# Row sums and scale spreading of the norms moved from VectorE to one-column and repeated-column products on TensorE

## The chip, the cores and the metric

The kernel runs on one core of a Trainium2 chip. The metric is the device time of one launch in microseconds (us). An engine is called by its short name in the profile: PE is TensorE's matmul (PEld its weight loads), DVE is VectorE, ACT is ScalarE, POOL is GpSimd, SP is SyncE, which here only issues DMAs.

## The reference

Two layers of a trunk on an activation `x` of 512 tokens by 1024 features, in float32. Per layer:

```python
x = x + 0.5 * swiglu(rms_norm(x, ffn1_norm), w_gate, w_up, w_down)     # D_FF 2816
h = rms_norm(x, mix_norm)
a, g, q, k, v = split(h @ w_in)
conv_out = silu(rms_norm(depthwise_conv31(a * sigmoid(g)) + conv_b, conv_norm))
diff_out = differential_attention(rms_norm(q), rms_norm(k), v, rel_bias, lam)   # 4 heads
x = x + concat(conv_out, diff_out) @ w_out
x = x + 0.5 * swiglu(rms_norm(x, ffn2_norm), w_gate, w_up, w_down)

def rms_norm(x, g):
    return x * rsqrt(mean(x * x, axis=-1) + 1e-6) * g
```

`lam` comes from four small vectors per layer: the exponentials of two dot products, and a constant.

## The kernel before

**Layout.** Features lie on the 128 partitions and tokens along the free axis: `x` is 8 tiles of 128 x 512. Most products are made three times (`mm3`, lines 160 to 167): weights and activations are split into a rounded high part (`whi`, `acth`, made by ACT or DVE) and the rest (`wlo`, `actl`), both in the format fp32r, and high x high, high x low and low x high are added up in PSUM. Weights come in through a ring of 5 raw buffers (`chunk`, `gather`, `sums`, lines 103 to 158). One product of 128 x 128 weights with 512 columns takes some 0.23 us of PE. Attention and its transposes use plain float32 products.

**The norms.** The gain of a norm goes into `acth` and `actl`; the scale of each token (one over the root of the mean square) is applied to the products afterwards. `Prep` (lines 252 to 275) squares each tile on ACT and adds the squares on POOL into `ssum` (128 x 512: one partial sum per partition and token). To get from there to a scale per token that every partition has, two helpers are used:

- `rows_rstd` (line 217) turns the 4 blocks of 128 tokens with 4 transposes on PE into PSUM, so that the tokens lie on partitions; DVE adds the 128 columns of each block (line 225), scales and adds epsilon (line 226); POOL raises to the power -0.5 (`rsqrt`, line 214). The result `rc` is 128 x 4: one number per token.
- `spread` (line 230) puts each column of `rc` on the diagonal of a 128 x 128 matrix (DVE, line 241) and multiplies a matrix of ones with it on PE (line 245), which leaves each token's scale in all partitions; ACT copies it to SBUF as `rb` (line 249). With `split=True` the number is first split into two fp32r parts (lines 234 and 236), two diagonals are made, and two fp32r products; else it is one product of 128 x 512 in float32.

Both are used eight times: for the four feed-forward blocks (split), for the input norm of the two mixers (not split), and for the norm over the channels of the convolution (`conv_finish`, line 690, not split), which sits in the last part of the mixer, where the last attention steps, the convolution's activation (tanh on ACT line 696, products on POOL line 694 and DVE lines 697 and 699) and the first output products meet.

**The order of the work.** Each engine works through its own queue in order. The order in each queue is not that of the Python text: a planner (`schedule_with_timeline_sim=True` in `kernel`) orders the instructions by its own estimate of when each can start, bound by data and by buffers: a tile with a `tag` and `bufs=n` has n buffers, and the next tile of the tag waits until an older one is done with. `keep_in_program_order` pins some instructions. In the very first feed-forward block the row sums are pinned before the fifth of eight accumulation steps of the third pair's first product group, and the spread before the fourth step of its second group (the call in `ffn`); in a mixer `first_products` pins both inside the second pair's products (`early`); in the three other feed-forward blocks and in `conv_finish` neither is pinned and the planner places them among the products.

**Buffers that the change touches.** The diagonals have the tag `diag` with one buffer (and a second one of the tag `sq`). The tile `lamv` of `make_scalars` (line 508 on) has the tag `diag` too. `make_scalars` is run once per layer's `lam`: a DMA from POOL's queue (line 513) spreads 4 x 64 numbers over all partitions, POOL multiplies (line 515, twice), DVE adds (line 517), ACT takes the exponential (line 519), DVE subtracts (line 521). `make_bias` (line 486 on) builds the table of the position bias with two small products (line 497), whose results DVE scales (line 498).

**The start.** Nine products of ones run while the first DMAs fly. Then `x` and the weights of the first two pairs arrive in three pieces (lines 189 to 198); ACT and DVE split them as they come, and PE follows.

Of the kernel before, what the change touches and what calls it, by code (L numbers as in the profile page):

```python
# [11 lines left out]
F32 = mybir.dt.float32  # L12
# [6 lines left out]
P = 128  # L19
# [48 lines left out]
def trunk(ctx: ExitStack, tc: tile.TileContext, xt, par, lamv, relb, onehot,  # L68
# [12 lines left out]
    def f32(ap):  # L81
        return ap.bitcast(F32)
# [3 lines left out]
    def bank(tag, name):  # L86
        return psum.tile([P, 512], F32, tag=tag, name=name, bufs=BANKS[tag])
# [124 lines left out]
    def rsqrt(v, n, use=""):  # L212
        y = small.tile([P, n], F32, tag=f"rs_y{n}{use}", name="rs_y")
        G.tensor_tensor(y, v, mhalf[:, :n], op=ALU.pow)
        return y

    def rows_rstd(s, dim, use="", pin=False):

        ps = bank("y", "ps_rows")
        for j in range(NT):  # L220
            mm = T.transpose(ps[:, j * P : (j + 1) * P], s[:, j * P : (j + 1) * P], ident)
            if pin:
                tc.keep_in_program_order(mm)
        v = small.tile([P, NT], F32, tag=f"rowv{use}", name="rowv")
        V.tensor_reduce(v, ps.rearrange("p (j c) -> p j c", j=NT), axis=AX.X, op=ALU.add)
        V.tensor_scalar(v, v, 1.0 / dim, EPS, op0=ALU.mult, op1=ALU.add)
        return rsqrt(v, NT, use), v

    def spread(rc, tag, pin=False, split=False):

        parts, dt, left = [rc], F32, ones
        if split:
            hi = small.tile([P, NT], F32R, tag="rc_hi", name="rc_hi")
            V.tensor_scalar(hi, rc, 1.0, None, op0=ALU.mult)
            lo = small.tile([P, NT], F32, tag="rc_lo", name="rc_lo")
            V.tensor_tensor(lo, rc, f32(hi), op=ALU.subtract)
            parts, dt, left = [f32(hi), lo], F32R, ones_r
        ps = bank("y", "ps_spread")
        for n, part in enumerate(parts):
            dg = tmp.tile([P, NT, P], dt, tag=("diag", "sq")[n], name="diag", bufs=1 + n)  # L240
            V.tensor_tensor(
                dg, ident.unsqueeze(1).broadcast_to([P, NT, P]),
                part.unsqueeze(2).broadcast_to([P, NT, P]), op=ALU.mult,
            )
            mm = T.matmul(ps, left, dg.rearrange("p j c -> p (j c)"), start=n == 0, stop=n == len(parts) - 1)
            if pin:
                tc.keep_in_program_order(mm)
        r = act.tile([P, SEQ], F32, tag=tag, name=tag)
        S.activation(r, ps, AF.Copy)
        return r  # L250

    class Prep:
# [30 lines left out]
    def products(pr, w, ps, i, at=None, amid=None):  # L283

        got = None
        for k in range(KT):
            if k == at:
                got = amid()
            mm3(ps, wpart(w[i], k), pr[k], k == 0, k == KT - 1, pin=at is not None and k in (0, at))
        return got  # L290
# [11 lines left out]
    def first_products(pr, w, ps, early=False):  # L302


        if not early:
            rc, v = rows_rstd(pr.s, DM)
            r = spread(rc, "rb", split=True)
        for k in range(KT):
            if early and k == STATS_AT:
                rc, v = rows_rstd(pr.s, DM, pin=True)  # L310
            for i in range(2):
                mm3(ps[0][i], wpart(w[0][i], k), pr[k], k == 0, k == KT - 1, pin=early and k in (0, STATS_AT))
        for i in range(2):
            for k in range(KT):
                if early and i == 0 and k == STATS_AT:
                    r = spread(rc, "rb", pin=True)
                mm3(ps[1][i], wpart(w[1][i], k), pr[k], k == 0, k == KT - 1, pin=early and k in (0, STATS_AT))
        return rc, v, r
# [95 lines left out]
    def ffn(pr, gu, dn, after, lead=None, aside=None):  # L414
        with tc.tile_pool(name="ffn", bufs=1) as fp:
            r = halves = None
            for m0, many in PARTS:
                hh, held, late = [], [], []

                def gated(n, us):  # L420
                    hi = fp.tile([P, SEQ], F32R, tag=f"hh{n}", name="hh")
                    lo = fp.tile([P, SEQ], F32R, tag=f"hl{n}", name="hl")
                    S.activation(hi, us, AF.Copy)
                    V.tensor_tensor(lo, us, f32(hi), op=ALU.subtract)
                    hh.append((hi, lo))

                def finish():
                    if late:
                        n, rest = late.pop()
                        gated(n, rest())  # L430

                for mm in range(many):
                    m = m0 + mm
                    if m == 4 and aside:
                        aside()
                    if m >= PLAIN:
                        w = sums(gu[m, 0], gu[m, 1])
                        late.append((mm, seven(halves, w, pair_banks(m), fp, finish, mm == many - 1)))
                        continue
                    w = lead[m] if lead and m < 2 else [chunk(gu[m, 0]), chunk(gu[m, 1])]  # L440
                    held.append((mm, w, pair_banks(m)))
                    if m == 0:
                        continue
                    if m == 1 and lead:
                        lead_products(pr, [h[1] for h in held], [h[2] for h in held])
                        continue
                    if m == 1:
                        _, _, r = first_products(pr, [h[1] for h in held], [h[2] for h in held])
                    elif r is None:
                        rc = products(pr, w, held[-1][2][0], 0, 4, lambda: rows_rstd(pr.s, DM, pin=True)[0])  # L450
                        r = products(pr, w, held[-1][2][1], 1, 3, lambda: spread(rc, "rb", pin=True, split=True))
                    else:
                        for i in range(2):
                            products(pr, w, held[-1][2][i], i)
                    for n, _, ps in held:
                        gs = fp.tile([P, 2, SEQ], F32, tag="gn", name="gs", bufs=2)
                        us = gs[:, 1]
                        V.tensor_tensor(gs[:, 0], ps[0], r, op=ALU.mult)
                        S.activation(gs[:, 0], gs[:, 0], AF.Silu)
                        V.tensor_tensor(us, ps[1], r, op=ALU.mult)  # L460
                        V.tensor_tensor(us, us, gs[:, 0], op=ALU.mult)
                        gated(n, us)
                    held = []
                    if not halves:
                        halves = Halves(fp, pr, r)
                finish()
                if m0 == 0:
                    halves.settle()
                blocks = [divmod(m0 + kk, HALF) for kk in range(many)]
                blocks = [(half, m * HALF + f) for m in range(KT) for half, f in blocks]  # L470
                w = None
                for m in range(KT):

                    ps = bank(turn_tag(m0 + many + m // 2), "ps_d")
                    for kk in range(many):
                        b = m * many + kk
                        if b % 8 == 0:
                            w = gather(dn, blocks[b : b + 8])
                        mm3(ps, wpart(w, b % 8), hh[kk], kk == 0, kk == many - 1)
                    V.scalar_tensor_tensor(x[:, m, :], ps, 0.5, x[:, m, :], op0=ALU.mult, op1=ALU.add)  # L480
                    if m0 + many == FT:
                        after(m)
# [58 lines left out]
    def mixer(l, pr, after):  # L541
        with tc.tile_pool(name="mix", bufs=1) as mp, tc.tile_pool(name="mt", bufs=2) as mt:
# [144 lines left out]
                conv_square(c, ys[c])  # L687

            def conv_finish():
                rcv = spread(rows_rstd(csum, CC, "c")[0], "rb")  # L690
                for c in range(CT):
                    z = ys[c]
                    hg = ghalf[l][:, c : c + 1]
                    G.tensor_tensor(z, z, rcv, op=ALU.mult)
                    th = mt.tile([P, SEQ], F32, tag="gl", name="th", bufs=1)
                    S.activation(th, z, AF.Tanh, scale=hg)
                    V.scalar_tensor_tensor(z, th, 1.0, z, op0=ALU.add, op1=ALU.mult)
                    S.activation(ch[:, c, :], z, AF.Copy, scale=hg)
                    V.scalar_tensor_tensor(cl[:, c, :], z, hg, f32(ch[:, c, :]), op0=ALU.mult, op1=ALU.subtract)
# [232 lines left out]
```

## Time and profile before

| | |
|---|---|
| median of 3 runs | 1796.49 us (1795.98 to 1796.54) |
| the profiled execution | 1796.31 us, its span 1794.5 us |
| PE busy | 1784.6 us, 99% of the span |
| DVE, ACT, POOL busy | 1211.1, 896.1 and 653.6 us |
| row sums' transposes (line 221) | 32 on PE |
| spread products (line 245) | 16 records on PE |
| sums on DVE (line 225) | 8 of 692 ns |
| diagonals on DVE (line 241) | 12 of 685 to 691 ns |
| ACT copy of the scale (line 249) | 8 of 598 ns |
| TensorE clock granted | full speed throughout |

A busy share is a share of the whole span. PE's ends are modelled and overlap, so PE's true pace is read from the distance between the starts of neighbouring products, not from the durations. A record in the tables is one instruction as the chip ran it; a float32 product appears as two of them.

### The profile page before, as it was taken

How to read it: one execution, taken by the hardware profiler on the slowest of the kernel's cores; microseconds unless marked ns; L12 is line 12 of the kernel's file. 1: busy time of each engine (PE TensorE's matmuls, PEld its weight loads, DVE VectorE, ACT ScalarE, POOL GpSimd, SP SyncE). 2: the span in 40 equal slices, each digit the busy share in tenths (PEclk: the TensorE clock that was granted, in tenths of full speed). 3: DMA queues.
4: the chain of work that ended last, by engine and by line, in shares of the span. 5: the costliest groups of instructions: out<-in, count | busy, mean ns of one | idle time of the engine just before them, and what ended most of it. 6: DMA issues, size and time to landing. Idle time of an engine off the chain costs nothing.

```text
span 1794.5 us, 28356 instructions
## 1 busy us (share of the span) xinstructions
PE 1784.6 (99%) x10845; PEld 1590.1 (89%) x10845; DVE 1211.1 (67%) x1863; ACT 896.1 (50%) x1482; POOL 653.6 (36%) x460
## 2 busy tenths in 40 slices
PE   9999999999999999999999999999999999999999
PEld 7899899888788899899888998998887888998997
DVE  6976477568867867477576765765788587673762
ACT  6555265445744456256433643654558354552651
POOL 4242232269843132133102312412797331322420
PEclk9999999999999999999999999999999999999999
DMA  7466476323212366466333654663231133664651
GB/s 243 107 179 183 108 181 176 118 94 94 71 48 83 94 165 188 106 171 189 105 94 98 171 167 120 177 179 118 71 114 51 48 106 91 166 178 112 180 150 59
DMA packets 111721, 231.24 MB, mean 129 GB/s; under 512 B 12151, under 2 KB 33414, under 8 KB 111584
## 3 DMA queue, kind: packets, MB, share of 16 engines
q1 hardware_dynamic: 91488, 191.93, 33.4%
q0 software_dynamic: 19808, 37.33, 12.5%
q8 instruction: 85, 1.39, 0.3%
q14 instruction: 52, 0.43, 0.1%
q10 hardware_dynamic: 288, 0.16, 0.0%
HBM read 227.26 MB, written 3.42 MB: 129 GB/s over the span
## 4 chain that ended last, share of the span: by engine, by line
PE 96%; DVE 2%; issue 1%; ACT 1%; DMA 0%; SPq 0%; ACTq 0%; DVEq 0%
PE ps_pair L384 38%; PE ps_d L166 9%; PE ps_d L163 9%; PE ps_d L167 9%; PE ps_pair L167 5%; PE ps_pair L166 5%; PE ps_pair L163 5%; PE ps_pair L596 2%; PE ps_pair L597 2%; PE ps_pair L598 2%; PE ps_out L163 1%; PE ps_out L166 1%; PE ps_sc L714 1%; PE ps_out L167 1%; DVE actl L263 1%; PE ps_v L628 1%
## 5 line engine op out<-in xcount | busy, mean ns | idle before, releaser
L100 ACT ACTIVATE whi<-wraw 128x1024 fp32r<-128x1024 f32 (+2 forms) x599 | 465.9, 802 | 609.5 <-PE ps_pair L384 225.7
L101 DVE TENSOR_TENSOR wlo<-wraw,whi 128x512 fp32r<-128x512 f32 (+2 forms) x556 | 526.0, 968 | 212.6 <-ACT whi L100 208.4
L384 PE MATMUL ps_pair<-acth,wlo 128*128 128x256 f32 x1088 | 308.5, 284 | 0.0
L384 PE MATMUL ps_pair<-actl,whi 128*128 128x256 f32 x1088 | 308.5, 284 | 0.0
L384 PE MATMUL ps_pair<-acth,whi 128*128 128x256 f32 x1088 | 308.4, 283 | 0.0
L166 PE MATMUL ps_d<-hl,whi 128*128 128x512 f32 x704 | 274.2, 390 | 0.0
L167 PE MATMUL ps_d<-hh,wlo 128*128 128x512 f32 x704 | 273.4, 390 | 0.0
L163 PE MATMUL ps_d<-hh,whi 128*128 128x512 f32 x704 | 268.7, 390 | 0.0
L384 PE MATMUL ps_pair<-th,wlo 128*128 128x256 f32 x816 | 231.3, 283 | 0.0
L384 PE MATMUL ps_pair<-tl,whi 128*128 128x256 f32 x816 | 231.2, 283 | 0.0
L384 PE MATMUL ps_pair<-th,whi 128*128 128x256 f32 x816 | 231.2, 283 | 0.0
L146 POOL TENSOR_TENSOR wraw<-wraw 128x512 f32<-128x512 f32 x68 | 101.8, 1497 | 339.5 <-DMA wraw<-in_gu 272.2
L141 POOL DMA_DIRECT2D wraw<-in_gu x68 | 82.0, 1207 | 392.4 <-DMA wraw<-in_gu 228.6
L384 PEld LDWEIGHTS ps_pair<-acth,whi 128*128 128x128 f32 x1088 | 209.1, 192 | 0.3
L384 PEld LDWEIGHTS ps_pair<-actl,whi 128*128 128x128 f32 x1088 | 209.0, 192 | 0.3
L384 PEld LDWEIGHTS ps_pair<-acth,wlo 128*128 128x128 f32 x1088 | 209.1, 192 | 0.0
L480 DVE SCALAR_TENSOR_TENSOR x<-ps_d,x 128x512 f32<-128x512 f32 x96 | 64.7, 689 | 179.6 <-PE ps_d L167 179.3
L166 PE MATMUL ps_pair<-actl,whi 128*128 128x512 f32 x448 | 175.0, 391 | 0.3
L163 PE MATMUL ps_pair<-acth,whi 128*128 128x512 f32 x448 | 174.4, 394 | 0.5 <-ACT whi L100 0.3
L167 PE MATMUL ps_pair<-acth,wlo 128*128 128x512 f32 x448 | 174.5, 391 | 0.0
L384 PEld LDWEIGHTS ps_pair<-tl,whi 128*128 128x128 f32 x816 | 156.7, 192 | 0.7
L384 PEld LDWEIGHTS ps_pair<-th,whi 128*128 128x128 f32 x816 | 156.7, 192 | 0.6
(176 smaller groups left out, 3268.9 us busy)
## 6 DMA issues: line engine op xcount, KB each, us to landing
wraw<-in_gu SPq DMA_DIRECT2D x208, 256.0 KB, 4.0
wraw<-in_gu SPq DMA_DIRECT2D x104, 512.0 KB, 3.7
wraw<-in_gu POOLq DMA_DIRECT2D x68, 512.0 KB, 5.7
wraw<-in_wqkv SPq DMA_DIRECT2D x24, 512.0 KB, 3.7
wraw<-in_dn SPq DMA_DIRECT2D x84, 128.0 KB, 3.1
wraw<-in_dn SPq DMA_DIRECT2D x32, 256.0 KB, 3.1
wraw<-in_wag SPq DMA_DIRECT2D x16, 512.0 KB, 3.6
wraw<-in_wout SPq DMA_DIRECT2D x16, 512.0 KB, 3.6
```

The lines of the kernel that those rows point to most:

```text
L100: S.activation(hi, raw, AF.Copy)
L101: (eng or V).tensor_tensor(out=lo, in0=raw, in1=f32(hi), op=ALU.subtract)
L141: nc.gpsimd.dma_start(two.rearrange("p (b c) -> p b c", b=2), u[:, h[0]].unsqueeze(1).broadcast_to([P, 2, 512]), accum_op=ALU.add)
L146: G.tensor_tensor(more[:, h[0]], two[:, h[1]], whole[:, h[0]], op=ALU.add)
L163: first = T.matmul(ps, wh, xh, start=start, stop=False)
L166: T.matmul(ps, wh, xl, start=False, stop=False)
L167: T.matmul(ps, wl, xh, start=False, stop=stop)
L384: mm = T.matmul(ps, l, r, start=first and i == j == 0, stop=False, skip_group_check=True)
L480: V.scalar_tensor_tensor(x[:, m, :], ps, 0.5, x[:, m, :], op0=ALU.mult, op1=ALU.add)
L596: T.matmul(ps[n], xh[:, t], wh, start=k == 0, stop=False)
L597: T.matmul(ps[n], xh[:, t], wl, start=False, stop=False)
L598: T.matmul(ps[n], xl[:, t], wh, start=False, stop=k == KT - 1)
```

## The change

`rows_rstd` no longer transposes: for each block of 128 tokens the block of `ssum` is the stationary operand and a single column of ones is streamed through, which sums over the partitions and leaves 128 x 1 in PSUM. DVE then reads 128 x 4 instead of 128 x 512, and the sum on DVE (line 225) falls away. `spread` makes no diagonals and no split: for each block the column of `rc`, repeated 128 times by its access pattern, is the stationary operand and the identity matrix (128 x 128) is streamed through; four float32 products of 128 columns take the place of one or two of 512. The scale, epsilon, power and the ACT copy stay. The tag `diag` is then used by `lamv` alone.

```diff
-    def rows_rstd(s, dim, use="", pin=False):
-        ps = bank("y", "ps_rows")
+    def rows_rstd(sums, dim, use="", pin=False):
+        ps = bank("y", "ps_rows")[:, :NT]
         for j in range(NT):
-            mm = T.transpose(ps[:, j * P : (j + 1) * P], s[:, j * P : (j + 1) * P], ident)
+            for n, s in enumerate(sums):
+                mm = T.matmul(ps[:, j : j + 1], s[:, j * P : (j + 1) * P], ones[:, :1],
+                              start=n == 0, stop=n == len(sums) - 1)
+                if pin:
+                    tc.keep_in_program_order(mm)
+        v = small.tile([P, NT], F32, tag=f"rowv{use}", name="rowv")
+        V.tensor_scalar(v, ps, 1.0 / dim, EPS, op0=ALU.mult, op1=ALU.add)
+        return rsqrt(v, NT, use), v
+    def spread_bank(rc, pin=False):
+        ps = bank("y", "ps_spread")
+        for j in range(NT):
+            mm = T.matmul(ps[:, j * P : (j + 1) * P], rc[:, j : j + 1].broadcast_to([P, P]), ident, start=True, stop=True)
             if pin:
                 tc.keep_in_program_order(mm)
-        v = small.tile([P, NT], F32, tag=f"rowv{use}", name="rowv")
-        V.tensor_reduce(v, ps.rearrange("p (j c) -> p j c", j=NT), axis=AX.X, op=ALU.add)
-        V.tensor_scalar(v, v, 1.0 / dim, EPS, op0=ALU.mult, op1=ALU.add)
-        return rsqrt(v, NT, use), v
-    def spread(rc, tag, pin=False, split=False):
-        parts, dt, left = [rc], F32, ones
-        if split:
...
-            parts, dt, left = [f32(hi), lo], F32R, ones_r
-        ps = bank("y", "ps_spread")
-        for n, part in enumerate(parts):
-            dg = tmp.tile([P, NT, P], dt, tag=("diag", "sq")[n], name="diag", bufs=1 + n)
-            V.tensor_tensor(
-                dg, ident.unsqueeze(1).broadcast_to([P, NT, P]),
-                part.unsqueeze(2).broadcast_to([P, NT, P]), op=ALU.mult,
-            )
-            mm = T.matmul(ps, left, dg.rearrange("p j c -> p (j c)"), start=n == 0, stop=n == len(parts) - 1)
-            if pin:
-                tc.keep_in_program_order(mm)
+        return ps
+    def spread(rc, tag, pin=False):
         r = act.tile([P, SEQ], F32, tag=tag, name=tag)
-        S.activation(r, ps, AF.Copy)
+        S.activation(r, spread_bank(rc, pin), AF.Copy)
         return r
...
-            r = spread(rc, "rb", split=True)
+            r = spread(rc, "rb")
...
-                        r = products(pr, w, held[-1][2][1], 1, 3, lambda: spread(rc, "rb", pin=True, split=True))
+                        r = products(pr, w, held[-1][2][1], 1, 3, lambda: spread(rc, "rb", pin=True))
...
-                rcv = spread(rows_rstd(csum, CC, "c")[0], "rb")
+                rcv = spread(rows_rstd([csum], CC, "c")[0], "rb")
```

More of the change, by code (lines that the diff above doesn't have):

```diff
@@ L227, in rows_rstd @@
-        return rsqrt(v, NT, use), v
-    def spread(rc, tag, pin=False, split=False):
-        parts, dt, left = [rc], F32, ones
-        if split:
[L233 to L236, printed above, removed]
-            parts, dt, left = [f32(hi), lo], F32R, ones_r
-        ps = bank("y", "ps_spread")
-        for n, part in enumerate(parts):
-            dg = tmp.tile([P, NT, P], dt, tag=("diag", "sq")[n], name="diag", bufs=1 + n)
-            V.tensor_tensor(
-                dg, ident.unsqueeze(1).broadcast_to([P, NT, P]),
-                part.unsqueeze(2).broadcast_to([P, NT, P]), op=ALU.mult,
-            )
-            mm = T.matmul(ps, left, dg.rearrange("p j c -> p (j c)"), start=n == 0, stop=n == len(parts) - 1)
-            if pin:
-                tc.keep_in_program_order(mm)
+        return ps
@@ L305, in first_products @@
         if not early:
-            rc, v = rows_rstd(pr.s, DM)
-            r = spread(rc, "rb", split=True)
+            rc, v = rows_rstd([pr.s], DM)
+            r = spread(rc, "rb")
         for k in range(KT):
             if early and k == STATS_AT:
-                rc, v = rows_rstd(pr.s, DM, pin=True)
+                rc, v = rows_rstd([pr.s], DM, pin=True)
             for i in range(2):
@@ L449, in ffn @@
                     elif r is None:
-                        rc = products(pr, w, held[-1][2][0], 0, 4, lambda: rows_rstd(pr.s, DM, pin=True)[0])
-                        r = products(pr, w, held[-1][2][1], 1, 3, lambda: spread(rc, "rb", pin=True, split=True))
+                        rc = products(pr, w, held[-1][2][0], 0, 4, lambda: rows_rstd([pr.s], DM, pin=True)[0])
+                        r = products(pr, w, held[-1][2][1], 1, 3, lambda: spread(rc, "rb", pin=True))
                     else:
```

## The prediction

> **What bounds the kernel now.** I read the busy shares first, then the chain of work that ended last, then the rows of the two helpers, and last the few stretches where PE isn't gapless. The shares and the chain, from the page:
>
> ```profile
> span 1794.5 us, 28356 instructions
> ...
> PE 1784.6 (99%) x10845; PEld 1590.1 (89%) x10845; DVE 1211.1 (67%) x1863; ACT 896.1 (50%) x1482; POOL 653.6 (36%) x460
> ...
> PE 96%; DVE 2%; issue 1%; ACT 1%; DMA 0%; SPq 0%; ACTq 0%; DVEq 0%
> ```
>
> PE carries 96% of the chain, so a PE instruction put among the products costs its full spacing, and DVE work taken away is worth nothing except where DVE holds PE up. What the helpers cost PE is read from distances between starts. The first row sums (timeline, PE):
>
> ```profile
> 31.27 0.39 PE L167 MATMUL ps_pair<-acth,wlo 128*128 128x512 f32 x1
> 31.50 0.60 PE L221 MATMUL ps_rows<-ident,ssum 128*128 128x128 f32 x4
> 31.86 0.48 PE L163 MATMUL ps_pair<-acth,whi 128*128 128x512 f32 x1
> 32.17 0.39 PE L166 MATMUL ps_pair<-actl,whi 128*128 128x512 f32 x1
> ```
>
> From 31.27 to 32.17 are 0.90 us; two regular products at 0.23 leave 0.44 for four transposes, 0.11 each. Pieces of the chain give the other spacings:
>
> ```profile
> 36.90 0.73 PE ps_spread L245 x2
> 91.72 76.31 PE ps_pair L384 x636
> 370.40 0.86 PE ps_spread L245 x2
> 477.82 0.89 PE ps_o L744 x8
> ```
>
> The split spread took 0.73 at its first place (two products of 0.23 and a wait for a diagonal; at the other three feed-forward blocks they sit 0.23 apart from their neighbours, 0.46 in all); the float32 spread 0.86; eight records of a float32 product of 128 columns (four products) 0.89, 0.111 a record; a product of 256 columns 0.120.
>
> Not gapless are the start and the last part of each mixer. At the start (timelines of ACT, POOL and PEld, and the row of the `lamv` DMA):
>
> ```profile
> 13.22 2.67 ACT L100 ACTIVATE whi<-wraw 128x512 fp32r<-128x512 f32 x4
> 15.93 2.08 ACT L262 ACTIVATE acth<-x,par 128x512 fp32r<-128x512 f32 x3
> ```
> ```profile
> 26.37 1.06 ACT L100 ACTIVATE whi<-wraw 128x1024 fp32r<-128x1024 f32 x1 [0.51 <-PE ps_pair L166]
> ```
> ```profile
> 29.08 0.19 PEld L167 LDWEIGHTS ps_pair<-acth,wlo 128*128 128x128 f32 x1 [0.45 <-DVE wlo L101]
> ```
> ```profile
> DMA to landing us min/median/max: 3.5/3.5/3.6
> ```
>
> ACT works without a gap from 13.22 to 20.5, then squares at POOL's pace, and the split at 26.37 feeds the weights for which PE stands at 29.08: ACT is only 0.51 us ahead there. The mixer's end (busy time by stretch: stretch, length, PE, PEld, DVE, ACT, POOL, clock, DMA share, GB/s):
>
> ```profile
> 490.00:500.00 10.00, 9.71 (x67) 8.00 (x66) 9.79 (x37) 7.94 (x27) 4.59 (x5) 1.00 0.00 0
> 500.00:512.00 12.00, 10.49 (x58) 7.96 (x58) 12.00 (x39) 9.85 (x28) 4.63 (x6) 1.00 0.01 1
> ```
>
> DVE is full. At the spacings above, PE's instructions from 489.85 to 512.2 (22.35 us) come to 18.8 us, so PE loses some 3.5 us there, mostly to the convolution's steps (the longest, 1.26 us, at 501.73 for `acth`, line 698). The second mixer has the same figures at 1381 to 1403.
>
> **The change part by part.** The sum is made against the profiled execution, 1796.31 us (span 1794.5 and 1.8 around it; 0.18 under the median).
>
> *Row sums on PE.* Four transposes (0.44) become four float32 products, each with two weight loads of 128 columns and one column streamed: eight records. No row shows one column. Low end: from 256 to 512 columns a record grows by 0.108 (0.120 to 0.228), so it would shrink to 0.012 at one column, 0.1 in all: -0.34 a place. High end: loads don't overlap and each takes the 0.19 us of its own record: 1.52, +1.08 a place. I take 0.111, the spacing of transposes and of 128-column records alike: the nearest rows, equal though the work streamed differs, which points to the load as the floor. 0.89, +0.45 a place. Six places lie in gapless PE: +2.7 (-2.0 to +6.5). The two in `conv_finish` are counted below.
>
> The Trainium skill's page "TensorE: Matmul & The Clock Gate", section "Back-to-back issue gap", gives about 60 cycles, or 25 ns, for 1 to 64 columns in an isolated stream. By it, as an estimate, a place would cost 0.2 instead of 0.89, the six 1.4 less than before, and the total +0.3 instead of +4.4. No record here has fewer than 128 columns on full weights.
>
> *Spread on PE.* Four float32 products of 128 columns: 8 x 0.111 = 0.89. First block 0.73 to 0.89, +0.16; three feed-forward blocks 0.46 to 0.89, +1.29; two mixers 0.86 to 0.89, +0.06. Sum +1.5 (a repeated column as weights isn't in the trace; I take it for a load like any other. Low end 0.86 a place, which the same columns took as one float32 product: +1.3; high end 0.19 a record: +5.3).
>
> *DVE.* Gone are 8 sums of 0.69, 12 diagonals of 0.69 and 8 small splits of 0.17: 15 us. Outside `conv_finish` PE's products cover them, and the scale just comes 1.4 to 2.2 us earlier to a spread that is pinned or waits its turn: nothing. The cover isn't lost.
>
> *`conv_finish`.* Here DVE and the latency count: sum and diagonal were 1.38 us, the timeline's rows at 490.54 and 493.29. In the compiled order the spread also stands three value products and a group of transposes earlier, and ACT's copy two instructions earlier. I work the scale's copy out at 494.9 instead of 496.34: rows end 0.45 later, DVE's small step waits behind `ov` to 491.7, power to 492.8, spread behind one score product to 494.7. All four channels follow it one by one some 2.5 us apart, so the gain of 1.4 arrives, less 0.2 for products pushed back: -1.2 a mixer, -2.4. Ends: all 1.7 us of latency (-3.4) or the rows' extra 0.45 uncovered and no gain (+0.9).
>
> *The start: `lamv` moves.* With the diagonals gone nothing holds its buffer, and the planner moves both layers' chains from 37 to 58 us to the very start. On POOL two DMA issues (0.58 each), four products (0.65 each) before the squares' sums; on DVE two sums (0.28) and two differences (0.14); on ACT two exponentials (0.20), behind the first three and the eighth of the weight splits. SP's queue is unchanged; ACT loses two table loads of 1.28 at 49 to 54, which covers nothing PE waits for; the bias product (0.95) moves ahead of the spread, its input issued one POOL instruction earlier: nothing.
> First chain: POOL is free at 6.1, products to 7.45, DVE's sum to 7.8, exponential to 8.05 instead of ACT going on at 6.37. ACT catches up by 10.8, since the next tile lands at 11.2 whatever it does. Nothing, but 128 KB ahead of that tile at some 300 GB/s: +0.3.
> Second chain: POOL reaches the DMA issue at 10.3. It lands in 3.5 us by the row above; the engines were then 60% busy, here 100% (1.04 of share, 400 GB/s from 12 to 20), where `x` took 5.4: I take 4.4. Then 1.3 for products, 0.3 sum, 0.4 for exponential and signals: 16.7. ACT stands before it from 13.9, 2.8 us late; less the 0.51 ahead, PE's wait at 29.08 grows by 2.3. Queued behind DVE's sum are four `wlo` and three `actl`, behind ACT's exponential three `whi` and three `acth`, then all squares; PE reaches them just late enough (17.5 on). With the 0.3, +2.6. Ends: landing in 1.9 (the fastest on POOL's queue, `oneh`) 0.3; in 5.7 (the median of POOL's large ones) 3.9.
>
> Sum: +2.7 +1.5 -2.4 +2.6 = +4.4; 1796.31 + 4.4 = 1800.7 us.
>
> **The rivals.**
> A. *A one-column product is cheap* (the low end). For it: the slope with columns. Against: the equal 0.111 of transposes and 128-column records. -2.0 in place of +2.7: 1796.0, no slower. It decides once a record costs under 0.02 us; below 0.094 the loss is under 0.2%. The page's rule above, 25 ns, would be this rival.
> B. *DVE's relief empties the mixers' ends.* DVE is full in just the 22 us where PE loses 3.5. If all of it comes back, -7.1 in place of -2.4: 1796.0, no slower. Against: the four channels run one after another on one `th` buffer, so only the start moves. It decides where a mixer gains over 3.4.
> C. *Loads don't overlap* when nothing streams between them: 0.19 a record, 6.5 in place of 2.7: 1804.5. Against: every row's spacing is under its load's 0.19.
> D. *The start doesn't stall*, the second `lamv` lands within 2 us: 1798.4. For it: `oneh` did. Against: both `lamv` rows, on a less busy DMA.
>
> **How the numbers follow.** Forecast 56%, its own range 1797.5 to 1804; A 14%, B 12%, C 10%, D 8%. A difference under 0.2% (3.6 us) is about what a measurement tells from none. Slower than 1800.1: 0.7 of the forecast and all of C, 0.49. Faster than 1792.9: a third of A and a fifth of B, 0.07. Same: the rest, 0.44. The range leaves out C's upper half and the faster thirds of A and B: 1795 to 1804.5.
>
> **What would show it.** Starts in the changed trace: eight one-column records taking about 0.9 us out of the stream (A 0.1, C 1.5); spread 0.89 everywhere; ACT idle before the second exponential until 16 to 17 us and PE's wait near 29 grown to about 3; `rb` in the mixer's end 1.4 us nearer to its row sums. Wrong would make me most of all a one-column record far from 0.11, or the planner's new order in the mixers' ends, where attention and convolution interleave differently, costing or saving more than the 1.2 worked out.

## The result and the profile after

The changed kernel takes 1802.57 us (median of 6 runs, 1802.33 to 1804.19), the kernel before 1796.45 beside it: ratio 1.0038, 95% interval 1.0028 to 1.0048, so 6.1 us slower. The forecast was 1800.7 with a range of 1795.0 to 1804.5. The profiled execution of the changed kernel is the slowest of the six, 1804.19 with a span of 1802.4, and has a stretch of half clock at the start, told below; its granted clock is 0.999, that of the other five, which lie between 1802.33 and 1803.08, is 1.000.

Page of the changed kernel, span, busy shares and chain by engine:

```profile
span 1802.4 us, 28487 instructions
...
PE 1790.9 (99%) x10925; PEld 1600.3 (89%) x10925; DVE 1201.6 (67%) x1835; ACT 894.3 (50%) x1480; POOL 646.3 (36%) x460
...
PE 94%; DVE 3%; ACT 1%; issue 1%; POOL 1%; DMA 1%; ACTq 0%; DVEq 0%; POOLq 0%
```

PE has 80 records more and is busy 6.3 us longer; DVE's busy time fell by 9.5 us (the forecast had 15) without making the kernel shorter. The chain of work that ended last, first of the changed kernel, then of before, each cut to pieces that have a counterpart in the other:

```profile
96.18 76.31 PE ps_pair L378 x636
...
...
482.80 0.89 PE ps_o L738 x8
551.01 1.22 DVE wlo L101
641.80 76.31 PE ps_pair L378 x636
989.18 76.31 PE ps_pair L378 x636
```
```profile
546.23 1.22 DVE wlo L101
636.14 76.31 PE ps_pair L384 x636
982.62 76.31 PE ps_pair L384 x636
```

The first two pieces start at 91.72 and 477.82 in the chain of before. The differences are where the time came from:

| stretch | distance to before at its end | grew by | forecast |
|---|---|---|---|
| start, with the first block's row sums and spread | +4.46 | 4.46 | 3.2 |
| first mixer's row sums and spread | +4.98 | 0.52 | 0.48 |
| first mixer's end (`conv_finish`) | +4.78 | -0.20 | -1.2 |
| second feed-forward block | +5.66 | 0.88 | 0.88 |
| next layer's first feed-forward block | +6.56 | 0.90 | 0.88 |

The second layer repeats it: +0.55 in the mixer's front, -0.10 in its end, +0.87 in the last block. The mixers' fronts and the feed-forward blocks are as forecast. The mixers' ends are not, and the start has 1.3 more than forecast in this one execution.

**Row sums and spread in gapless PE** (timeline of the changed kernel, PE, start and duration):

```profile
366.49 0.39 PE L167 MATMUL ps_pair<-acth,wlo 128*128 128x512 f32 x1
366.72 0.95 PE L223 MATMUL ps_rows<-ones,ssum 128*128 128x1 f32 x8
367.53 0.49 PE L163 MATMUL ps_pair<-acth,whi 128*128 128x512 f32 x1
367.85 0.40 PE L166 MATMUL ps_pair<-actl,whi 128*128 128x512 f32 x1
```

From 366.49 to 367.85 are 1.36 us; less two regular products of 0.23 the eight one-column records took 0.90, 0.11 each. The forecast had 0.89, from records of 128 columns.

**The start** (changed kernel: row of the `lamv` DMA, ACT and PE from the timelines):

```profile
DMA to landing us min/median/max: 4.1/5.1/6.1
```
```profile
16.73 0.20 ACT L513 ACTIVATE lame<-lamd 128x2 f32<-128x2 f32 x1 [3.31 <-DVE lamd L511]
```
```profile
27.80 0.39 PE L167 MATMUL ps_pair<-acth,wlo 128*128 128x512 f32 x1
29.18 0.51 PE L163 MATMUL ps_pair<-acth,whi 128*128 128x512 f32 x1 [0.99 <-ACT whi L100]
29.52 0.39 PE L166 MATMUL ps_pair<-actl,whi 128*128 128x512 f32 x1
31.36 0.50 PE L167 MATMUL ps_pair<-acth,wlo 128*128 128x512 f32 x1 [1.45 <-DVE wlo L101]
31.70 0.50 PE L163 MATMUL ps_pair<-acth,whi 128*128 128x512 f32 x1
32.00 0.63 PE L166 MATMUL ps_pair<-actl,whi 128*128 128x512 f32 x1
32.43 0.63 PE L167 MATMUL ps_pair<-acth,wlo 128*128 128x512 f32 x1
```

ACT stands 3.31 us before the second exponential and PE waits 0.99 and 1.45 us for the weight splits that come behind it, 2.4 in all (before: 0.45 at 29.08). The last two lines stand 0.43 apart where regular products stand 0.23 apart, and so it goes on to 34.99: PE at about half its pace for 3 us. The granted clock from 32 to 35 is 0.50. The ten products from 31.36 to the row sums at 35.35 took 3.99 us, where the run with the move alone, below, needed 2.39 for ten: 1.6 us lost, which more than covers the 1.3.

### The profile page after: what moved, and what is told of

The parts are those of the page before. It is cut to its first block, busy times and chain, and to the rows that moved or that the text cites. A ratio compares the mean times of both kernels' runs of the same rounds, so it can differ in the third digit from the quotient of the medians.

```text
span 1802.4 us, 28487 instructions
## 1 busy us (share of the span) xinstructions
PE 1790.9 (99%) x10925; PEld 1600.3 (89%) x10925; DVE 1201.6 (67%) x1835; ACT 894.3 (50%) x1480; POOL 646.3 (36%) x460
## 4 chain that ended last, share of the span: by engine, by line
PE 94%; DVE 3%; ACT 1%; issue 1%; POOL 1%; DMA 1%; ACTq 0%; DVEq 0%; POOLq 0%
PE ps_pair L378 38%; PE ps_d L166 9%; PE ps_d L163 9%; PE ps_d L167 9%; PE ps_pair L167 5%; PE ps_pair L166 5%; PE ps_pair L163 5%; PE ps_pair L591 2%; PE ps_pair L592 2%; PE ps_pair L590 2%; PE ps_sc L708 1%; PE ps_out L163 1%; PE ps_out L167 1%; PE ps_out L166 1%; DVE actl L257 1%; PE ps_v L622 1%
```

## The experiments

All medians are against the kernel before on the same chip: 1796.09 for the first four runs, 1796.05 for the next seven, 1796.20 for the last.

**The parts apart.** First the move of the scalars' chains alone, on the kernel before:

```diff
-SPACE = 392
+SPACE = 376
...
-            t = tmp.tile([P, SEQ], F32, tag="diag", name="lamv", bufs=1)
+            t = tmp.tile([P, 6 * HD], F32, tag="lamv", name="lamv", bufs=1)
```

> The kernel before with one edit: lamv gets a buffer of its own (SBUF was 64 bytes too full for it, so the bias table's spare columns shrink from 392 to 376), so that the chains of both layers' scalars start at the very beginning as in the changed kernel; row sums and spread stay as they were. Forecast's step: the second lamv transfer holds up ACT's weight splits and PE's wait near 29 us grows by some 2.3, in all +2.6 over the kernel before. From the changed kernel's trace: its first long group starts 4.46 later, of which 0.6 are the first block's row sums and spread and some 1.6 a stretch of half clock in that execution, so +2.3, and about +3.9 in an execution with the slow stretch. Rival (the move is free, the time at the start comes from something else, such as the helpers' new order): +0.3 or less.

Measured: 1798.83, +2.7 (ratio 1.0016, 1.0007 to 1.0025). Its chain passes the first long group at 93.79 and keeps that distance of 2.0 to 2.1 to before to the end, and it contains the transfer and the splits behind it:

```profile
9.35 6.03 DMA lamv<-in_lamv
16.67 1.57 ACT whi L100 x3
```

The profiled execution took 1798.33. Three of the eleven show a granted clock of 0.999 and took 1799.59 to 1800.43, which points to the half clock in some executions here too. The move costs 2.0 to 2.7 without any of the new products; the rival that it is free falls.

Next, the changed kernel with the chains held back by another buffer:

```diff
-            t = tmp.tile([P, SEQ], F32, tag="diag", name="lamv", bufs=1)
+            t = tmp.tile([P, SEQ], F32, tag="sq", name="lamv")
```

> The changed kernel with one edit: lamv takes a buffer of the squares' rotation instead of the diagonals' unused one, which holds the scalars' chains back until squares are done; everything else is as in the change. If the move costs 2.3 to 2.6 by itself, this is the changed kernel less that: +3.6 to +3.9 over the kernel before, and no half clock at the start, since PE never stands still long enough. By the forecast's sum, whose conv_finish term was -2.4, it would be +1.8. Rival (the move is free): as the changed kernel, +6.1.

Measured: 1799.99, +3.9 (1.0022, 1.0014 to 1.0031): 2.2 less than the whole change, and not the +1.8 of the forecast's sum. The first mixer's end got 0.17 shorter by its chain (478.86 and 547.10 stand at +1.04 and +0.87).

The new row sums alone, with the scalars' chains where the diagonals hold them before, and the new spread alone, with the chains behind the squares. One of the eight places in each run; the comments say which functions stand there:

```python
rcv = spread(rows_rstd([csum], CC, "c")[0], "rb")   # row sums alone: new rows_rstd, old spread
...
rcv = spread(rows_rstd(csum, CC, "c")[0], "rb")     # spread alone: old rows_rstd, new spread
```

> The kernel before with the new row sums alone (one-column products with ones in all eight places); the spread by diagonals stays and with it the place of the scalars' chains. Forecast: six gapless places at +0.45 are +2.7; in conv_finish DVE's sum of 0.69 goes and PE pays 0.45, so 0 to -0.5 for both mixers, together +2.2 to +2.7. From the changed kernel's trace (0.90 us a place out of the stream where transposes took 0.44; mixers' ends hardly gaining): +2.7 to +3.0. Rival A (one column is cheap): -2. Rival (the two parts hinder each other and neither costs this alone): under +2.

> The kernel before with the new spread alone (repeated columns of weights times the identity in all places), the old row sums by transposes and DVE, and the scalars' chains held back as in the run with them held. Forecast: +1.5 in gapless places (0.16 at the first block, 0.43 at three feed-forward blocks, 0.03 at two mixers), and in conv_finish the diagonal's 0.69 off the latency, -0.7 a mixer, together about +0.1. From the changed kernel's trace, whose mixers' ends got only 0.1 to 0.2 shorter with both parts, of which the row sums' extra 0.45 is in the way: +0.3 to +1.3. The sum of this run and of the one with row sums alone should be that of the run with the chains held, if the parts add.

Measured: row sums 1797.91, +1.8 (1.0010, 1.0002 to 1.0019); spread 1797.25, +1.2 (1.0006, 0.9997 to 1.0015). The sum, 3.0, is 0.9 under the run with both; the intervals reach 1.6 us to either side, so the times alone don't show that the parts fail to add. By the chains the places agree with their price of 0.45 and 0.43 in the feed-forward blocks (636.54 and 983.49 in the chain of the row sums stand at +0.40 and +0.87, 636.10 and 983.02 in that of the spread at -0.04 and +0.40), and the first mixer's end gained 0.27 with the row sums, 0.22 with the spread, and 0.17 with both (the second 0.20, 0.13 and 0.07): the two gains don't add. That is 0.3 a mixer of the 0.9. The rest lies at the start, and single profiles don't settle it: the first group of 636 starts at 91.72 in the profile of before, and at 91.75, 91.36 and 91.31 in three runs below that differ from it only in the mixers.

**What prices a record.** One column against 128 columns, on the run with the chains held:

```diff
-        ps = bank("y", "ps_rows")[:, :NT]
+        ps = bank("y", "ps_rows")
...
-                mm = T.matmul(ps[:, j : j + 1], s[:, j * P : (j + 1) * P], ones[:, :1],
+                mm = T.matmul(ps[:, j * P : (j + 1) * P], s[:, j * P : (j + 1) * P], ones,
...
-        V.tensor_scalar(v, ps, 1.0 / dim, EPS, op0=ALU.mult, op1=ALU.add)
+        V.tensor_scalar(v, ps[:, ::P], 1.0 / dim, EPS, op0=ALU.mult, op1=ALU.add)
```

> As the run with the scalars' chains held, with one edit: the row sums' products stream all 128 columns of ones instead of one, and VectorE reads every 128th column of the result; still eight records a place. If the loads of the 128-column weights set a record's price, the eight cost 8 x 0.111 (the spread's records) instead of 8 x 0.099, +0.1 a place, +0.6 to +0.8 over the run with the chains held. Rival A's slope (a record shrinks with its columns, from 0.108 less per 256 columns) would make a one-column record 0.054 shorter than a 128-column one: 0.43 a place, +2.6 in six places.

Measured: 1799.91 against 1799.99 (+3.86 and +3.90, each over the kernel before beside it). Its PE timeline:

```profile
362.40 0.39 PE L167 MATMUL ps_pair<-acth,wlo 128*128 128x512 f32 x1
362.63 1.05 PE L223 MATMUL ps_rows<-ones,ssum 128*128 128x128 f32 x8
363.44 0.48 PE L163 MATMUL ps_pair<-acth,whi 128*128 128x512 f32 x1
363.75 0.40 PE L166 MATMUL ps_pair<-actl,whi 128*128 128x512 f32 x1
```

1.35 us from 362.40 to 363.75, as with one column (1.36). From 1 to 128 columns the streamed columns cost nothing; rival A's slope falls. Each record has its own load of 128 columns of weights in both variants, and that is what they have in common; a run with narrower weights was not made. The only narrower loads in the trace of before, four columns for the bias, take 0.08 us against 0.19, but the two records of 128 columns that go with two of them took 0.31 us together (53.26 to 53.57), not less than 0.11 each. So that the load sets the price is argued, not shown.

**Why the start pays.** The changed kernel with a second buffer for the second layer's `lamv`:

```diff
-SPACE = 392
+SPACE = 376
...
-            t = tmp.tile([P, SEQ], F32, tag="diag", name="lamv", bufs=1)
+            t = tmp.tile([P, SEQ if l == 0 else 6 * HD], F32, tag="diag" if l == 0 else "lamv", name="lamv", bufs=1)
```

> The changed kernel with one edit: the second layer's lamv has a buffer of its own, so that its transfer is issued right behind the first instead of after the first chain's sums (the bias table's spare columns shrink from 392 to 376 for the space). The chains stay at the very start. Forecast's mechanism (ACT stands before the second exponential because that transfer is issued at 9.5 to 10.3 and lands at 15.6): it lands by about 12, ACT hardly waits, and 1.8 to 2.5 of the 2.6 at the start go; total +3.6 to +4.3 over the kernel before, and no half clock. Rival (the start pays for the extra instructions and the 128 KB each ahead of the weights): as the changed kernel, +6.1.

Measured: 1800.08, +4.0 (1.0021, 1.0011 to 1.0031), where the whole change was +6.1. ACT's exponentials (timeline):

```profile
9.28 0.19 ACT L513 ACTIVATE lame<-lamd 128x2 f32<-128x2 f32 x1
11.57 0.19 ACT L513 ACTIVATE lame<-lamd 128x2 f32<-128x2 f32 x1
```

No idle time stands before either, PE is gapless from 24 to 32 us, and the first long group starts at 92.26, 0.54 behind before, which is the first block's row sums and spread (0.61 by the forecast). The chains are still at the very start and work as much; the second transfer left POOL at 2.5 instead of 9.5 (the planner also put PE's first products in a slightly different order). So it was the late transfer that made the move dear, not its instructions.

**The mixers' ends.** The disputed term by itself: the new row sums and spread (`rows_new`, `spread_new`) in `conv_finish` alone, on the kernel before:

```diff
-                rcv = spread(rows_rstd(csum, CC, "c")[0], "rb")
+                rcv = spread_new(rows_new([csum], CC, "c")[0], "rb")
```

> The kernel before with the change made in conv_finish alone: one-column row sums and the new spread there, everything else as before. This is the term that the forecast put at -1.2 a mixer, -2.4 in all: 1793.7. From the chains of the runs with everything changed and the scalars' chains held, whose mixers' ends got 0.17 and 0.12 shorter: -0.3, 1795.8.

Measured: 1795.96, -0.1 (1.0001, 0.9992 to 1.0010); by its chain the two ends are 0.17 and 0.06 shorter. The -2.4 falls: the interval's low end is -1.4. But the scale did come earlier. ACT's timeline in this run, the scale's copy, the first channel's tanh and the last channel's `acth`:

```profile
495.30 0.61 ACT L278 ACTIVATE rb<-ps_spread 128x512 f32<-128x512 f32 x1
...
497.68 0.72 ACT L725 ACTIVATE th<-yp,ghalf 128x512 f32<-128x512 f32 x1
...
508.75 0.72 ACT L727 ACTIVATE acth<-u,ghalf 128x512 fp32r<-128x512 f32 x1
```

The same three in the timeline of before:

```profile
496.34 0.58 ACT L249 ACTIVATE rb<-ps_spread 128x512 f32<-128x512 f32 x1
...
498.80 0.73 ACT L696 ACTIVATE th<-yp,ghalf 128x512 f32<-128x512 f32 x1
...
509.36 0.72 ACT L698 ACTIVATE acth<-u,ghalf 128x512 fp32r<-128x512 f32 x1 [0.90 <-DVE u L697]
```

The surroundings stand at the same place within 0.04 (the value products of 477.82 at 477.86). So the scale is 1.04 earlier, the first channel 1.12, the last only 0.61. And PE's waits from 489 to 513 (the view of waits; engine, line, what it waited for, total, times, longest), of before and of this run:

```profile
PE ps_out L163 <- ACT acth L698: 1.3, 1, 1.3
PE ps_o L744 <- ACT at L737: 0.2, 1, 0.2
```
```profile
PE ps_out L163 <- DVE mn L747: 0.6, 1, 0.6
PE ps_at L764 <- ACT at L766: 0.2, 1, 0.2
```

The wait of the first output product for the convolution's `acth` is gone; in its place that product waits 0.6 us for DVE (`mn`), which reads out a bank of attention's scores late; the output products take turns with those scores in the banks `sc` and `po` (a bank is one of the kernel's buffers in PSUM). The waits listed come to 1.5 before and 0.8 now. Most of the 0.7 went to PE's own new records: eight instead of four for the row sums (+0.46), and 0.89 for 0.86 in the spread.

That made a theory: the bank, not the scale, holds the product now. It was tried with one edit, which lets the first output group write the bank that the spread leaves free, once on the changed kernel with the chains held and once on the kernel before:

```diff
-                    ps = bank(("sc", "po")[m % 2], "ps_out")[:, : t.stop - t.start]
+                    tag = "y" if half == m == 0 else ("sc", "po")[m % 2]
+                    ps = bank(tag, "ps_out")[:, : t.stop - t.start]
```

> The changed kernel with the scalars' chains held and one more edit: the first product of the mixer's last matrix writes the bank that the spread has left free, instead of one that attention's scores use in turn; PE's order up to that product stays the same. Theory (the earlier scale no longer helps because the product now waits for a score bank that VectorE reads out late): the 0.62 us wait ahead of it goes, it starts when ScalarE has acth ready, about 1.0 earlier, and some 0.3 to 0.6 a mixer come off: 1798.8 to 1799.4. Rival (ScalarE's acth or PE's own order sets it): no change from 1799.99.

> The kernel before with only that free bank for the first product of the mixer's last matrix. There the product waits 1.26 us for acth, which the scale sets, and not for a bank: the theory says no change at that product, 1796.1 within 0.3. If banks bind the mixer's end in any case: -0.6 to -1.2.

Measured: 1797.18 against 1799.99 without the edit (2.8 less, 1.4 a mixer), and on the kernel before 1793.30, -2.75 (0.9987, 0.9978 to 0.9996). The first is more than twice what the theory allowed, and the second breaks it: with the late scale of before the same edit brings just as much. PE's timeline of that second run:

```profile
501.37 0.73 PE L163 MATMUL ps_out<-acth,whi 128*128 128x512 f32 x2 [1.26 <-ACT acth L698]
...
505.04 0.85 PE L163 MATMUL ps_out<-acth,whi 128*128 128x512 f32 x3
...
507.89 0.85 PE L163 MATMUL ps_out<-acth,whi 128*128 128x512 f32 x3
...
510.41 0.94 PE L163 MATMUL ps_out<-acth,whi 128*128 128x512 f32 x3
```

The wait for the first `acth` is still 1.26 us, untouched. What changed is the number behind the x: three products are there each time a channel after the first arrives, where the timeline of before has two:

```profile
507.39 0.73 PE L163 MATMUL ps_out<-acth,whi 128*128 128x512 f32 x2
...
510.39 0.71 PE L163 MATMUL ps_out<-acth,whi 128*128 128x512 f32 x2
```

With three output groups open instead of two, each arriving channel gives PE nine products instead of six. In the 12.2 us from the same place PE starts 65 records (499.64 to 511.84) where the kernel before starts 58 (500.00 to 512.20). So the mixer's end depends on how much work is open per channel while the channels come 2.5 to 3 us apart, and not only on when the first one comes. For the change this leaves a reckoning that fits but that no run isolates: the last channel 0.6 earlier, less 0.46 of added PE work, is 0.15 a mixer, and 0.17 and 0.06 were measured. Why the last channel kept only 0.6 of 1.04 was not tried; its steps share DVE's and ACT's queues with attention.

One run on the same question told little. The channels were scaled by a number that is there long before, so this kernel leaves out the convolution's own scale and computes something else:

```diff
-                rcv = spread(rows_rstd(csum, CC, "c")[0], "rb")
+                spread(rows_rstd(csum, CC, "c")[0], "rb", aside=True)
+                rcv = row["b"]
```

> The kernel before with one edit in conv_finish: the four channels are multiplied by the mixer's first scale, which is long there, instead of by the convolution's own; row sums, diagonals, spread and its copy are all still done, into a buffer that nobody reads. So the convolution's normalisation is left out, its work is not, and only the wait for the scale is gone, where the change brings the scale 1.1 earlier. If the scale's arrival sets the mixer's end, as the forecast's conv_finish term has it (-1.2 for 1.4), most of the 3.5 PE loses there comes back: -4 to -7 for both mixers. If attention's own chain of scores, exponentials, copies and banks is right behind it, as the waits of the changed kernel suggest: -0.5 to -2 for both.

Measured: 1803.68, +7.6 (1.0043, 1.0030 to 1.0055), which neither side expected. The planner moved the first channels up among the softmaxes: the first tanh starts at 467.6 instead of 498.8. PE's two longest waits from 466 to 515 then are:

```profile
PE ps_sc L715 <- DVE e L729: 2.1, 3, 1.5
PE ps_sc L715 <- DVE mn L719: 1.6, 1, 1.6
```

The granted clock fell to 0.83 from 480 to 490 in this profile, but executions at 1.000 took just as long (1803.68 and 1803.71), so the clock isn't what makes the run slow. It doesn't decide between the scale and the banks, since the order changed with the wait. The two waits point to the channels' steps on DVE, which, taken early, hold up attention's scores by more than they free.

**A version from what the runs showed.** A place costs PE its records. Outside `conv_finish` the sum over partitions and its spread can be one record, a product of 512 columns with a full matrix of ones:

```diff
+    def rsum_bank(s, tag, dim, pin=False):
+        ps = bank("y", "ps_sum")
+        mm = T.matmul(ps, ones_r, s, start=True, stop=True)
+        if pin:
+            tc.keep_in_program_order(mm)
+        r = act.tile([P, SEQ], F32, tag=tag, name=tag)
+        V.tensor_scalar(r, ps, 1.0 / dim, EPS, op0=ALU.mult, op1=ALU.add)
+        V.reciprocal(r, r)
+        S.activation(r, r, AF.Sqrt)
+        return r
```

> A version built on what the runs show so far, that a place costs PE its records times 0.10 to 0.23 whatever they hold. In the six places outside conv_finish the sum over partitions and its spread are one fp32r product of 512 columns with a full matrix of ones, one record of 0.23; the scale is then worked out on all 512 columns by VectorE (two steps) and a square root on ScalarE, and the last square's sum is rounded to fp32r. The mixers keep their transposes for the per-row scale. conv_finish has the old row sums and the new spread. PE saves 4 x (0.90 - 0.23) in feed-forward blocks, 2 x (0.86 - 0.23) in mixers and some 0.2 in each mixer's end: -4.3, 1791.8. Rival (the square root's function loads on ScalarE and the longer steps bring the scale too late for the products' results): 0 or slower.

Measured: 1794.37, -1.7 (0.9991, 0.9982 to 1.0000). In its chain each feed-forward block is 0.73 shorter (635.09 and 980.84 stand at -1.05 and -1.78) and the mixer's front 0.65, as expected, but the mixer lost 0.85 behind that (396.63 at -1.16, 545.92 at -0.31). Why was not taken apart; DVE's reciprocal of 3.35 us and two loads of ACT's function tables of 1.28 each are new there.

The last run keeps `rsum_bank` for the feed-forward blocks alone and adds the free bank and, in `conv_finish`, the new spread on the old row sums:

```diff
-                G.tensor_tensor(self.s, self.s, sq, op=ALU.add)
+                if k == KT - 1 and self.gain.startswith("ffn"):
+                    self.sr = tmp.tile([P, SEQ], F32R, tag="diag", name="ssumr", bufs=1)
+                G.tensor_tensor(self.s if self.sr is None else self.sr, self.s, sq, op=ALU.add)
...
+                        r = products(pr, w, held[-1][2][0], 0, 4, lambda: rsum_bank(pr.sr, "rb", DM, pin=True))
+                        products(pr, w, held[-1][2][1], 1)
...
+                    tag = "y" if half == m == 0 else ("sc", "po")[m % 2]
```

> What the runs point to, on the kernel before: in the four feed-forward blocks the direct row sum (one fp32r product of 512 columns, then two steps on VectorE and a square root on ScalarE), which took 0.73 off each block in the run that had it everywhere; in the mixers the old transposes and diagonals at their starts, the new spread in conv_finish (0.2 each), and the free bank for the first product of the mixer's last matrix (2.75 in all). If the parts add: -0.67 x 4, -0.4, -2.75, together -5.8, 1790.3. Rival (the gains in the mixers' ends share one stretch and don't add, or ScalarE's function loads cost as in the run with the direct sum in the mixers too): -3 to -4, 1792 to 1793.

Measured: 1790.44, ratio 0.9969 (0.9958 to 0.9981): 5.8 faster than the kernel before and 12 faster than the change. The parts add to within 0.2.

## Why the prediction was right, and where it was not

- *PE bounds, DVE's work is worth nothing outside the mixers' ends*: held. The gapless stretches grew by PE's new records, though DVE was 9.5 us less busy.
- *Row sums, +2.7*: held. 0.90 us a place (0.89 forecast) and 0.9 per feed-forward block together with the spread. The run with 128 columns shows why the neighbouring 128-column records were the right rows, and the slope from 512 to 256 columns the wrong one. The Trainium skill's page "TensorE: Matmul & The Clock Gate", section "Back-to-back issue gap", gives 25 ns for short isolated products, against 0.11 us measured, so the measurement decides and rival A is out. The same section puts sustained pairs of load and product at about 81 ns for 128 columns, which is nearer; the trace has 0.11 for these float32 records.
- *Spread, +1.5*: held, a repeated column loads like any other (0.89 at every place but the first, where the chain has 1.09 right behind the bias product; with the chains held it is 0.89 there too).
- *The start, +2.6*: held in size and mechanism: +2.7 alone, 2.1 to 2.2 taken back by holding the chains or by the second buffer. That the exponential ended at 16.9 as forecast (16.7) is luck: the DMA was issued earlier (9.5 for 10.3) but took 6.1 us for 4.4, and POOL's two products took 0.6 for 1.3. PE's waits there came to 2.4 instead of about 3. The 0.3 for 128 KB ahead of a tile at 300 GB/s should have been 0.44 by its own figures, and no run shows the term by itself. Rival D, no stall, is out: it needs the transfer to leave early, as in the run with two buffers.
- *`conv_finish`, -2.4*: wrong by 2.1, more than the whole 1.9 us between forecast and result. Two steps failed. The scale was to come 1.4 earlier and came 1.04 earlier (in the changed kernel 1.08 nearer to its row sums). And "All four channels follow it one by one some 2.5 us apart, so the gain of 1.4 arrives, less 0.2 for products pushed back" didn't hold: the last channel kept 0.6 of it, the wait at the first output product passed from `acth` to a score bank, and 0.46 of new PE work filled the rest. Measured alone it is worth 0.1 in all, inside the ends of the bound (-3.4 to +0.9 for both mixers), where -2.4 had been taken. Rival B, all idle time back, is further off still.
- *Rival C, loads don't overlap*, 0.19 a record: out at 0.11. Its time of 1804.5 counted the row sums alone; the spread's records at the same price would have put it 3.8 higher.

Sum with the measured terms: rows and spread 4.3 (0.6 at the start, 0.52, 0.55, 0.88, 0.90, 0.87), move 2.0 to 2.7, mixers' ends -0.3, together 6.0 to 6.7; measured 6.1.

## What to carry to other kernels

Price small products by the spacing of records with the same weight load, not by their columns: one streamed column cost as much as 128. When a change drops a buffer's other users, look what else had that tag: a tile that was held back may start early, and one small late transfer in front of in-order queues then cost about half as much as all the new products. And before crediting an earlier input with its time, look at the next wait at that place (here PSUM banks shared with other work) and at how much work each arriving piece opens; one bank more was worth 1.4 us where an input 1.04 earlier was worth 0.1.

## What the runs showed of the hardware that was not expected

- *The clock after a gap.* In the profiled execution of the change PE ran two products in the 3.6 us between 27.80 and 31.36, and from 32.00 to 34.99 its products stood 0.427 apart instead of 0.23. The run with the chains' move alone has nearly the same gap in its profile, 3.4 us (two products between 27.73 and 31.12), and products 0.23 apart behind it, so the gap is not always enough. The Trainium skill's page "TensorE: Matmul & The Clock Gate", part on the HAM clock gate, says that the clock halves after an idle window of about 3.4 us and that the window runs free of the kernel, so that the same gap may or may not hold one; neither profile contradicts that, though PE was not wholly idle in either gap. In the run without the convolution's scale the granted clock was 0.50 from 483 to 485, and PE's longest gap ahead of it was 1.64 us, so a PE that is little used for some us may be enough; no run isolates that.
- *A small transfer on a busy system.* The 128 KB of `lamv` took 3.5 us from issue to landing when the profile of before issued them late, and 6.1 at 9.5 us, while weights stream in; the first, issued at 1.3, took 4.1.
- *A reciprocal is long.* DVE's reciprocal of 128 x 512 takes 3.35 us (row of the last run), nearly five times the scaling step beside it:

```profile
L268 DVE RECIPROCAL rb<-rb 128x512 f32<-128x512 f32 x4 | 13.4, 3353 | 0.1
L267 DVE TENSOR_SCALAR rb<-ps_sum 128x512 f32<-128x512 f32 x4 | 2.8, 692 | 8.9 <-PE ps_sum L263 8.9
```
